# A hybrid decoder's gelus: square, tanh and VectorE steps replaced by ScalarE's gelu function

## The chip, the cores and the metric

One core of one Trainium2 chip runs the kernel. The metric is the device time of one execution in microseconds; the times below are medians of several executions. All matmuls and all vector work are in float32 (a first part of the first layer uses a split into two float32r halves).

## The reference

Two layers, each on 512 tokens of width 1024. Cut to what the change touches:

```python
h  = rg_lru(causal_conv(xr, ...), ...)          # recurrent branch
yr = h * jax.nn.gelu(gr)                        # gr: its gate branch
...
act = jax.nn.gelu(jnp.einsum('cd,ced->ce', xc, uc))   # 128 experts of each token
out = jnp.einsum('ce,ced->cd', gc * act, vc)          # gc: softmax over the chosen scores
```

`jax.nn.gelu` is here the tanh form, 0.5 x (1 + tanh(sqrt(2/pi) (x + 0.044715 x^3))). For each token and each of 8 heads a product-key search chooses 16 of 16384 experts; an expert is one row of `peer_u` and one row of `peer_v`. Around these stand differential attention (8 heads), two LayerNorms per layer (their square roots on ScalarE), softmax exponentials and sigmoids (computed as tanh).

## The kernel before, in words

Tokens lie in 4 blocks of 128 partitions. Three generators are merged into one program order by a clock of due times in `run` (L897 to L913): `gathers` walks the experts of every layer and block, `dense` walks the mixer and the routing of the four plans (a layer and a pair of blocks each, `PLAN`), and `late` chooses the experts of each plan's second block. Within the mixer `weave` alternates attention with the recurrent branch. The steps are emitted in that order; the framework may then place instructions of one engine a little earlier or later, and each engine runs its own queue in order.

`experts` (L785) takes two experts at a time (G=2, "a pair", 64 pairs per block and layer, 512 in all). For each expert GpSimd gathers 128 rows of u and v (L831, 1 MB per gather) into one of 8 buffers of the tag "uv", and VectorE multiplies the u half with x and sums it into one column of `dots` (L834, which also multiplies by C_GELU). After the second of the pair, ScalarE squares both columns (L842) and takes a tanh of each column by itself (L844, since scale and bias of that tanh are the column of `dots`); VectorE multiplies `dots` with the gate `g` into `w` (L846). The first step of the next pair then calls `finish` (L792): VectorE makes `w = (q + 1) * w` (L794), and each of the two experts is added either by VectorE into `acc` (L801) or by TensorE into `pv`, which needs a diagonal matrix made by ScalarE (L805) and two matmuls (L807, four in the trace). The buffer of an expert is free only after that, and the next gather into it waits for this.

Which of the two engines adds an expert is chosen by `Load`, a planner that sums a modelled cost of every emitted instruction for TensorE, VectorE and the DMAs: VectorE if `dve + 1.22 <= pe + 1.72`. It counts a VectorE instruction as 0.15 + n/960 us, n its elements per partition.

`lru` (L461) does a group of 128 channels in each of 8 turns per plan: conv, gates by tanh (L492), a tanh and an exp (L498, L499), a square root (L505), a scan (L516), and then the gelu of the gate branch: square (L520), a VectorE step (L521), tanh (L523), a VectorE step (L524) and the product with the scan's result (L527).

`choose` (L732) ends with a softmax over the chosen 16: exp (L773), sum, reciprocal, a factor 0.5/C_GELU (L777), product into `g`.

ScalarE evaluates functions from a table that holds some functions at a time; a change of table is an instruction of its own in the trace, ACT_TABLE_LOAD, shown at the line of the operation that it stands before.

Of the kernel before, what the change touches and what calls it, by code (L numbers as in the profile page):

```python
# [12 lines left out]
F32 = mybir.dt.float32  # L13
# [4 lines left out]
AF = mybir.ActivationFunctionType  # L18
ALU = mybir.AluOpType
AX = mybir.AxisListType  # L20

P = 128
D = 1024
# [10 lines left out]
LN_EPS = 1e-5  # L34
RMS_EPS = 1e-6
NEG = -1.0e30
C_GELU = math.sqrt(2.0 / math.pi)
A_GELU = math.sqrt(0.044715)


CH_Q, CH_K, CH_V, CH_XR, CH_GR, CH_GA, CH_GB = 0, 8, 16, 24, 32, 40, 48
# [81 lines left out]
class Decoder:  # L123
# [337 lines left out]
    def lru(self, l, cst, blocks, x, yr):  # L461
        nc, t1, t2 = self.nc, self.t1, self.t2
        n = len(blocks) * P
        t0 = blocks[0] * P
        c, hb, sp4 = cst["c"], cst["hb"], cst["sp4"]
        W = MAXN
        cost = len(blocks) * C_CHUNK
        for g in range(KC):
            gw = t2.tile([P, 2, P], F32, name="gw", tag="gs")
            nc.sync.dma_start(gw, self.gpk[l, g].rearrange("p (a c) -> p a c", a=2))  # L470
            px = self.proj_T(l, CH_XR + g, x, n)
            xr = t1.tile([P, 3 + W], F32, name="xr", tag="xr")
            if t0 == 0:
                nc.vector.memset(xr[:, 0:3], 0.0)
            else:
                nc.vector.tensor_copy(xr[:, 0:3], self.hist[:, g, :])
            nc.scalar.copy(xr[:, 3 : 3 + n], px[:, :n])
            yield cost
            nc.vector.tensor_copy(self.hist[:, g, :], xr[:, n : n + 3])
            xc = t1.tile([P, W], F32, name="xc", tag="xc")[:, :n]  # L480
            tap = lambda k: c[:, CC_W + k * 8 + g : CC_W + k * 8 + g + 1]
            nc.scalar.activation(xc, xr[:, 0:n], AF.Identity, bias=c[:, CC_B + g : CC_B + g + 1],
                                 scale=tap(0))
            for k in range(1, 4):
                nc.vector.scalar_tensor_tensor(out=xc, in0=xr[:, k : k + n], scalar=tap(k), in1=xc,
                                               op0=ALU.mult, op1=ALU.add)
            tha = t1.tile([P, W], F32, name="tha", tag="tha")[:, :n]
            thx = t1.tile([P, W], F32, name="thx", tag="thx")[:, :n]
            for gi, th in enumerate((tha, thx)):
                pg = self.ps_mm.tile([P, 512], F32, name="pg", tag="mm")  # L490
                nc.tensor.matmul(pg[:, :n], gw[:, gi, :], xc, start=True, stop=True)
                nc.scalar.activation(th, pg[:, :n], AF.Tanh, scale=0.5,  # L492
                                     bias=hb[:, gi * 8 + g : gi * 8 + g + 1])
            yield 1.0
            pgr = self.proj_T(l, CH_GR + g, x, n)
            s4 = sp4[:, g : g + 1]
            tl = t1.tile([P, W], F32, name="tl", tag="tl")[:, :n]
            nc.scalar.activation(tl, tha, AF.Tanh, scale=s4, bias=s4)  # L498
            nc.scalar.activation(tha, tha, AF.Exp, scale=s4, bias=s4)  # L499
            mu = t1.tile([P, W], F32, name="mu", tag="mu")[:, :n]  # L500
            nc.scalar.activation(mu, tha, AF.Square)

            nc.vector.scalar_tensor_tensor(out=mu, in0=mu, scalar=1.0, in1=tl, op0=ALU.add,
                                           op1=ALU.mult)
            nc.scalar.activation(mu, mu, AF.Sqrt, scale=-1.0)  # L505
            if t0 == 0:
                nc.vector.memset(mu[:, 0:1], 1.0)
            yield cost
            nc.vector.scalar_tensor_tensor(out=thx, in0=thx, scalar=1.0, in1=xc, op0=ALU.add,
                                           op1=ALU.mult)  # L510
            nc.vector.scalar_tensor_tensor(out=mu, in0=thx, scalar=0.5, in1=mu, op0=ALU.mult,
                                           op1=ALU.mult)
            hh = thx
            if t0 == 0:
                nc.vector.memset(self.hst[:, g : g + 1], 0.0)
            nc.vector.tensor_tensor_scan(hh, tha, mu, self.hst[:, g : g + 1], ALU.mult, ALU.add)  # L516
            nc.vector.tensor_copy(self.hst[:, g : g + 1], hh[:, n - 1 : n])
            yield 0.5
            pg = pgr
            nc.scalar.activation(tl, pg[:, :n], AF.Square, scale=A_GELU)  # L520
            nc.vector.scalar_tensor_tensor(out=tl, in0=tl, scalar=1.0, in1=pg[:, :n], op0=ALU.add,  # L521
                                           op1=ALU.mult)
            nc.scalar.activation(tl, tl, AF.Tanh, scale=C_GELU)  # L523
            nc.vector.scalar_tensor_tensor(out=tl, in0=tl, scalar=1.0, in1=pg[:, :n], op0=ALU.add,  # L524
                                           op1=ALU.mult)
            y = tl if yr.split else yr.plain[:, g, :n]
            nc.vector.scalar_tensor_tensor(out=y, in0=tl, scalar=0.5, in1=hh, op0=ALU.mult,  # L527
                                           op1=ALU.mult)
            if yr.split:
                self.keep(yr, (slice(None), g, slice(0, n)), y)  # L530
            yield 1.0
# [200 lines left out]
    def choose(self, l, h0, HG, sv, si, b):  # L732

        nc, t2 = self.nc, self.t2
# [36 lines left out]
        st = t2.tile([P, max(HGS[False])], F32, name="sm_st", tag="sm_st")[:, :HG]  # L771
# [1 line left out]
        nc.scalar.activation(ef, ef, AF.Exp)  # L773
        nc.vector.tensor_reduce(st, ef, AX.X, ALU.add)
        nc.vector.reciprocal(st, st)

        nc.vector.tensor_scalar(st, st, 0.5 / C_GELU, None, ALU.mult)  # L777
        nc.vector.tensor_tensor(self.g[b][:, js].rearrange("p (h k) -> p h k", h=HG), ef,
                                st.unsqueeze(2).to_broadcast([P, HG, TOPK]), ALU.mult)
        for h in range(h0, h0 + HG):  # L780
# [4 lines left out]
    def experts(self, l, b, G=2):  # L785
        nc, pp = self.nc, self.pp
        x = self.xn[b]
        pv = None
        e, g = self.e[b], self.g[b]
        began = [False]  # L790

        def finish(j0, q, w, uvs):  # L792

            nc.vector.scalar_tensor_tensor(out=w, in0=q, scalar=1.0, in1=w, op0=ALU.add,  # L794
                                           op1=ALU.mult)
            for i in range(G):
                j, t = j0 + i, uvs[i]
                self.load.update()
                vector = self.load.dve + 1.22 <= self.load.pe + 1.72
                if j == P - 1 or (vector and j < P - 2):  # L800
                    nc.vector.scalar_tensor_tensor(out=acc, in0=t[:, D:], scalar=w[:, i : i + 1],  # L801
                                                   in1=acc, op0=ALU.mult, op1=ALU.add)
                else:
                    dg = pp.tile([P, P], F32, name="dg", tag="dg")
                    nc.scalar.activation(dg, self.ident, AF.Copy, scale=w[:, i : i + 1])  # L805
                    for half in range(2):
                        nc.tensor.matmul(pv[:, half], dg,  # L807
                                         t[:, D + half * 512 : D + (half + 1) * 512],
                                         start=not began[0], stop=j == P - 2)
                    began[0] = True  # L810
            yield

        prev = iter(())
        for j0 in range(0, P, G):
# [8 lines left out]
                    pv = self.ps_v.tile([P, 2, 512], F32, name="pv", tag="pv")  # L823
            dots = pp.tile([P, G], F32, name="dots", tag="dots")
            q = pp.tile([P, G], F32, name="q", tag="q")
            w = pp.tile([P, G], F32, name="w", tag="w")
            uvs = []
            for i in range(G):
                j = j0 + i
                t = self.gp.tile([P, 2 * D], F32, name="uvt", tag="uv")  # L830
                nc.gpsimd.indirect_dma_start(  # L831
                    out=t, out_offset=None, in_=self.uv,
                    in_offset=bass.IndirectOffsetOnAxis(ap=e[:, j : j + 1], axis=0))
                nc.vector.scalar_tensor_tensor(out=t[:, :D], in0=t[:, :D], scalar=C_GELU, in1=x,  # L834
                                               op0=ALU.mult, op1=ALU.mult,
                                               accum_out=dots[:, i : i + 1])
                uvs.append(t)
                if i == 0:
                    next(prev, None)
                else:  # L840

                    nc.scalar.activation(q, dots, AF.Square, scale=A_GELU / C_GELU)  # L842
                    for k in range(G):
                        nc.scalar.activation(q[:, k : k + 1], q[:, k : k + 1], AF.Tanh,  # L844
                                             scale=dots[:, k : k + 1], bias=dots[:, k : k + 1])
                    nc.vector.tensor_tensor(w, dots, g[:, j0 : j0 + G], ALU.mult)  # L846
                yield 1
            prev = finish(j0, q, w, uvs)
        for _ in prev:
            pass  # L850
        sums = pp.tile([P, 1], F32, name="sums2", tag="sums2")
# [96 lines left out]
```

## Time and profile before

| | |
|---|---|
| median of 3 runs | 3462.6 us (3461.32 to 3471.1) |
| profiled execution's own time | 3468.77 us |
| its span in the trace | 3466.6 us |
| TensorE busy | 2996.7 us (86%) |
| VectorE busy | 2717.2 us (78%) |
| ScalarE busy | 1329.1 us (38%) |
| GpSimd busy (issue of gathers) | 1303.2 us (38%) |
| moved by DMA | 1290.65 MB, 372 GB/s over the span |
| chain that ended last | PE 36%, DVE 25%, DMA 19%, issue 9%, ACT 5%, POOL 5% |

PE is TensorE, DVE VectorE, ACT ScalarE, POOL GpSimd, SP the queue of plain DMAs. Busy time is the union of an engine's instructions. The chain that ended last is followed back from the last instruction, at each step to what released it. An average over the span hides that the work has stages with different limits, so the rows below are read stage by stage.

In this document the stages go by their place in the span: the **first projections** (0 to 300 us, before the first gather), three **attention stages** (460 to 720, 1150 to 1500, 2000 to 2300), three **routing stages** (1000 to 1150, 1750 to 1900, 2600 to 2800), and **streaming stages**, mostly the rest, the longest of them the last (2800 to the end).

### The profile page before, as it was taken

How to read it: one execution, taken by the hardware profiler on the slowest of the kernel's cores; microseconds unless marked ns; L12 is line 12 of the kernel's file. 1: busy time of each engine (PE TensorE's matmuls, PEld its weight loads, DVE VectorE, ACT ScalarE, POOL GpSimd, SP SyncE). 2: the span in 40 equal slices, each digit the busy share in tenths (PEclk: the TensorE clock that was granted, in tenths of full speed). 3: DMA queues.
4: the chain of work that ended last, by engine and by line, in shares of the span. 5: the costliest groups of instructions: out<-in, count | busy, mean ns of one | idle time of the engine just before them, and what ended most of it. 6: DMA issues, size and time to landing. Idle time of an engine off the chain costs nothing.

```text
span 3466.6 us, 39937 instructions
## 1 busy us (share of the span) xinstructions
PE 2996.7 (86%) x11916; PEld 1916.2 (55%) x11916; DVE 2717.2 (78%) x7210; ACT 1329.1 (38%) x3730; POOL 1303.2 (38%) x1033
## 2 busy tenths in 40 slices
PE   8997999999997899999997799999998687656555
PEld 7996666667754466677653266677765232212111
DVE  7765888888689677777799668878779965678777
ACT  7852245543132344533222345444232233223222
POOL 0001233334333333344433433334433345555553
PEclk9998999999999899999998999999999889877777
DMA  6455899999999999999999999999999899999997
GB/s 203 161 173 208 318 407 383 395 418 418 418 394 373 368 383 375 399 416 408 418 403 345 404 384 384 391 412 418 418 416 352 315 385 421 422 422 405 422 422 317
DMA packets 219126, 1290.65 MB, mean 372 GB/s; under 512 B 24592, under 2 KB 37136, under 8 KB 87840
## 3 DMA queue, kind: packets, MB, share of 16 engines
q0 software_dynamic: 147456, 1073.81, 76.7%
q1 hardware_dynamic: 71456, 214.30, 16.3%
q8 instruction: 96, 1.57, 0.2%
q14 instruction: 118, 0.97, 0.1%
HBM read 1285.92 MB, written 2.10 MB: 372 GB/s over the span
## 4 chain that ended last, share of the span: by engine, by line
PE 36%; DVE 25%; DMA 19%; issue 9%; ACT 5%; POOL 5%; POOLq 0%; SPq 0%; DVEq 0%; ACTq 0%
DMA uvt<-uv_dram,e 19%; PE ps_mm L255 14%; PE pv L807 13%; DVE uvt L834 9%; POOL uvt L831 5%; DVE acc L801 4%; PE ps_mm L277 2%; ACT q L844 1%; PE ps_mm L665 1%; DVE oh L765 1%; PE ps_ln L315 1%; DVE ef L767 1%; DVE oh L762 1%; PE s L388 1%; PE po L419 1%
## 5 line engine op out<-in xcount | busy, mean ns | idle before, releaser
L831 POOL DMA_INDIRECT uvt<-uv_dram,e x1024 | 1300.6, 1270 | 2132.0 <-PE pv L807 721.5
L807 PE MATMUL pv<-uvt,dg 128*128 128x512 f32 x2796 | 1448.5, 657 | 355.2 <-ACT dg L805 352.6
L834 DVE SCALAR_TENSOR_TENSOR uvt<-uvt,xn 128x1024 f32<-128x1024 f32 x1024 | 1243.2, 1219 | 151.3 <-DMA uvt<-uv_dram,e 89.2
L807 PEld LDWEIGHTS pv<-uvt,dg 128*128 128x128 f32 x2796 | 541.2, 205 | 1081.3 <-ACT dg L805 576.9
L255 PE MATMUL ps_mm<-room_xT,w 128*128 128x256 f32 x2304 | 538.4, 381 | 0.7 <-ACT room_xT L287 0.7
L842 ACT ACTIVATE q<-dots 128x2 f32<-128x2 f32 x512 | 103.7, 202 | 1093.4 <-DVE uvt L834 1088.3
L255 PEld LDWEIGHTS ps_mm<-room_xT,w 128*128 128x128 f32 x2304 | 431.4, 190 | 107.1 <-issue 50.3
L801 DVE SCALAR_TENSOR_TENSOR acc<-uvt,w,acc 128x1024 f32<-128x1024 f32 x325 | 416.6, 1282 | 7.8
L805 ACT ACTIVATE dg<-ident,w 128x128 f32<-128x128 f32 x699 | 263.0, 397 | 261.8 <-DVE w L794 154.5
L844 ACT ACTIVATE q<-q,dots 128x1 f32<-128x1 f32 x1024 | 341.9, 379 | 15.1
L794 DVE SCALAR_TENSOR_TENSOR w<-q,w 128x2 f32<-128x2 f32 x512 | 80.8, 158 | 289.8 <-ACT q L844 279.0
L665 PE MATMUL ps_mm<-room_xT,w 128*128 128x256 f32 (+1 forms) x1056 | 243.5, 379 | 0.0
L665 PEld LDWEIGHTS ps_mm<-room_xT,w 128*128 128x128 f32 x1056 | 196.5, 196 | 46.2 <-issue 23.8
L240 DVE TENSOR_TENSOR wsp<-raw,wsp 128x1024 fp32r<-128x1024 f32 x80 | 97.1, 1221 | 23.4 <-ACT wsp L239 23.2
L277 PEld LDWEIGHTS ps_mm<-w,room_xT 128*128 128x128 f32 x768 | 92.1, 192 | 9.0 <-issue 8.0
L277 PE MATMUL ps_mm<-w,room_xT 128*128 128x128 f32 x768 | 94.5, 276 | 0.0
L277 PEld LDWEIGHTS ps_mm<-w,room_m 128*128 128x128 f32 x768 | 89.2, 192 | 9.6 <-issue 8.6
L846 DVE TENSOR_TENSOR w<-dots,g 128x2 f32<-128x2 f32 x512 | 80.1, 157 | 17.3 <-ACT dg L805 4.3
L315 PE MATMUL ps_ln<-lnrows,ident 16*128 16x512 f32 x96 | 63.1, 779 | 35.3 <-DVE w L846 22.6
L255 PE MATMUL ps_mm<-room_yr,w 128*128 128x256 f32 x384 | 90.6, 380 | 0.0
L277 PE MATMUL ps_mm<-w,room_m 128*128 128x128 f32 x768 | 89.7, 275 | 0.4 <-DVE mth L544 0.2
L255 PE MATMUL ps_mm<-room_ya,w 128*128 128x256 f32 x384 | 88.9, 379 | 0.0
(200 smaller groups left out, 3023.6 us busy)
## 6 DMA issues: line engine op xcount, KB each, us to landing
w<-wpk_dram SPq DMA_DIRECT2D x304, 512.0 KB
raw<-wpk_dram SPq DMA_DIRECT2D x80, 512.0 KB
uvt<-uv_dram,e POOLq DMA_INDIRECT x1024
gw<-gpk_dram SPq DMA_DIRECT2D x32, 128.0 KB
sk<-spk_dram SPq DMA_DIRECT2D x64, 64.0 KB
xn<-x_dram SPq DMA_DIRECT2D x4, 512.0 KB
out_dram<-xn SPq DMA_DIRECT2D x8, 256.0 KB
lq<-lqk_dram SPq DMA_DIRECT2D x2, 128.0 KB
```

The source lines that it names most:

```text
L240: self.nc.vector.tensor_tensor(lo, raw, hi.bitcast(F32), ALU.subtract)
L255: self.nc.tensor.matmul(ps[:, :n], w, x, start=i == 0, stop=i == len(steps) - 1)
L277: self.nc.tensor.matmul(out[:, i], x(slice(i * P, (i + 1) * P)), w, start=j == 0, stop=j == len(steps) - 1)
L315: self.nc.tensor.matmul(ps[:, half], self.ident[:16, r : r + 1].to_broadcast([16, P]), self.lnrows, start=True, stop=True)
L665: nc.tensor.matmul(pq[:, :n], w[:, kc, :], self.acts_x.plain[:, kc, t0 : t0 + n], start=kc == 0, stop=kc == KC - 1)
L801: nc.vector.scalar_tensor_tensor(out=acc, in0=t[:, D:], scalar=w[:, i : i + 1], in1=acc, op0=ALU.mult, op1=ALU.add)
L805: nc.scalar.activation(dg, self.ident, AF.Copy, scale=w[:, i : i + 1])
L807: nc.tensor.matmul(pv[:, half], dg, t[:, D + half * 512 : D + (half + 1) * 512], start=not began[0], stop=j == P - 2)
L831: nc.gpsimd.indirect_dma_start(out=t, out_offset=None, in_=self.uv, in_offset=bass.IndirectOffsetOnAxis(ap=e[:, j : j + 1], axis=0))
L834: nc.vector.scalar_tensor_tensor(out=t[:, :D], in0=t[:, :D], scalar=C_GELU, in1=x, op0=ALU.mult, op1=ALU.mult, accum_out=dots[:, i : i + 1])
L842: nc.scalar.activation(q, dots, AF.Square, scale=A_GELU / C_GELU)
L844: nc.scalar.activation(q[:, k : k + 1], q[:, k : k + 1], AF.Tanh, scale=dots[:, k : k + 1], bias=dots[:, k : k + 1])
```

## The change

In the experts, one gelu over both columns takes the place of the square and the two tanh; `w` becomes the plain product of that with `g`, made in `finish`. In the recurrent branch one gelu takes the place of square, VectorE step, tanh and VectorE step. The factors that belonged to the old form go (C_GELU in the dot product becomes 1.0, and the softmax loses its 0.5/C_GELU step).

```diff
@@ lru
-            pg = pgr
-            nc.scalar.activation(tl, pg[:, :n], AF.Square, scale=A_GELU)
-            nc.vector.scalar_tensor_tensor(out=tl, in0=tl, scalar=1.0, in1=pg[:, :n], op0=ALU.add,
-                                           op1=ALU.mult)
-            nc.scalar.activation(tl, tl, AF.Tanh, scale=C_GELU)
-            nc.vector.scalar_tensor_tensor(out=tl, in0=tl, scalar=1.0, in1=pg[:, :n], op0=ALU.add,
-                                           op1=ALU.mult)
+            nc.scalar.activation(tl, pgr[:, :n], AF.Gelu_apprx_tanh)
             y = tl if yr.split else yr.plain[:, g, :n]
-            nc.vector.scalar_tensor_tensor(out=y, in0=tl, scalar=0.5, in1=hh, op0=ALU.mult,
-                                           op1=ALU.mult)
+            nc.vector.tensor_tensor(y, tl, hh, ALU.mult)
@@ choose
-        nc.vector.tensor_scalar(st, st, 0.5 / C_GELU, None, ALU.mult)
@@ experts
-        def finish(j0, q, w, uvs):
-            nc.vector.scalar_tensor_tensor(out=w, in0=q, scalar=1.0, in1=w, op0=ALU.add,
-                                           op1=ALU.mult)
+        def finish(j0, q, uvs):
+            w = pp.tile([P, G], F32, name="w", tag="w")
+            nc.vector.tensor_tensor(w, q, g[:, j0 : j0 + G], ALU.mult)
...
-            w = pp.tile([P, G], F32, name="w", tag="w")
...
-                nc.vector.scalar_tensor_tensor(out=t[:, :D], in0=t[:, :D], scalar=C_GELU, in1=x,
+                nc.vector.scalar_tensor_tensor(out=t[:, :D], in0=t[:, :D], scalar=1.0, in1=x,
...
-                    nc.scalar.activation(q, dots, AF.Square, scale=A_GELU / C_GELU)
-                    for k in range(G):
-                        nc.scalar.activation(q[:, k : k + 1], q[:, k : k + 1], AF.Tanh,
-                                             scale=dots[:, k : k + 1], bias=dots[:, k : k + 1])
-                    nc.vector.tensor_tensor(w, dots, g[:, j0 : j0 + G], ALU.mult)
+                    nc.scalar.activation(q, dots, AF.Gelu_apprx_tanh)
...
-            prev = finish(j0, q, w, uvs)
+            prev = finish(j0, q, uvs)
```

## Rows read from the trace of the kernel before

**Rows 1.** Busy time by stage: stretch, length, each engine's busy us (instructions), clock, DMA share, GB/s.

```profile
0.00:300.00 300.00, 278.09 (x2168) 264.00 (x2169) 205.45 (x498) 191.92 (x378) 3.66 (x10) 0.98 0.47 158
...
460.00:720.00 260.00, 252.58 (x1105) 173.71 (x1104) 224.14 (x555) 136.72 (x373) 102.22 (x83) 1.00 0.99 396
...
1000.00:1150.00 150.00, 121.71 (x401) 72.14 (x400) 145.35 (x574) 43.66 (x151) 55.28 (x45) 0.93 0.94 365
1150.00:1500.00 350.00, 338.64 (x1262) 213.46 (x1260) 251.19 (x678) 165.21 (x475) 125.65 (x112) 0.97 0.98 389
...
1750.00:1900.00 150.00, 118.92 (x406) 72.17 (x405) 148.50 (x572) 41.51 (x144) 55.18 (x43) 0.90 0.96 375
...
2000.00:2300.00 300.00, 295.40 (x1203) 195.03 (x1202) 239.75 (x604) 149.91 (x415) 115.28 (x94) 1.00 0.99 390
...
2600.00:2800.00 200.00, 150.32 (x408) 77.56 (x407) 192.32 (x704) 54.84 (x184) 79.01 (x62) 0.88 0.88 333
2800.00:3466.00 666.00, 419.02 (x683) 142.62 (x682) 482.37 (x893) 186.89 (x567) 334.33 (x252) 0.82 0.98 405
```

**Rows 2.** Page, the span in 40 equal slices: GB/s of the DMAs.

```profile
GB/s 203 161 173 208 318 407 383 395 418 418 418 394 373 368 383 375 399 416 408 418 403 345 404 384 384 391 412 418 418 416 352 315 385 421 422 422 405 422 422 317
```

**Rows 3.** Chain of waits by line, in 50:150, 460:720, 1150:1500, 1750:1900, in that order.

```profile
by line: PE ps_mm L255 21.0%; PE ps_mm L277 12.1%; PE ps_qk L255 10.1%; ACT wsp L239 9.5%; PE pg L491 5.2%; ACT L523 4.4%; ACT pr L400 4.2%; ACT L505 3.8%; PE s L388 2.4%; DVE xc L485 2.3%; issue 2.0%; ACT xc L482 2.0%; PE po L419 1.8%; ACT
by line: DMA uvt<-uv_dram,e 38.8%; PE pv L807 10.7%; PE ps_mm L255 9.4%; issue 9.3%; DVE uvt L834 7.9%; DVE acc L801 4.7%; PE ps_mm L277 2.7%; POOL uvt L831 2.3%; DVE at_st L397 1.6%; DVE oh L762 1.5%; DVE oh L765 1.1%; PE s L388 1.1%; DVE 
by line: PE pv L807 39.7%; PE ps_mm L255 25.7%; PE ps_mm L277 6.4%; DVE uvt L834 4.0%; PE pg L491 3.0%; PE s L388 2.2%; DMA uvt<-uv_dram,e 2.1%; ACT q L844 1.3%; PE po L419 1.2%; issue 1.1%; DVE xc L485 0.9%; DVE oh L762 0.8%; DVE oh L765 0
by line: DVE uvt L834 31.7%; DVE acc L801 12.4%; issue 8.1%; DVE sc L730 4.8%; DVE si L727 4.8%; DVE top L727 4.7%; DVE sv L725 3.4%; DVE top L725 3.3%; DVE ef L767 3.3%; DVE ca L745 2.8%; PE pv L807 2.6%; PE ps_mm L665 2.3%; ACT q L844 2.2
```

**Rows 4.** Groups by line: busy us, mean ns of one, idle before and what ended it.

```profile
L842 ACT ACTIVATE q<-dots 128x2 f32<-128x2 f32 x512 | 103.7, 202 | 1093.4 <-DVE uvt L834 1088.3 <-issue 3.5 <-DVE mu L507 0.9
L844 ACT ACTIVATE q<-q,dots 128x1 f32<-128x1 f32 x1024 | 341.9, 379 | 15.1
L846 DVE TENSOR_TENSOR w<-dots,g 128x2 f32<-128x2 f32 x512 | 80.1, 157 | 17.3 <-ACT dg L805 4.3 <-issue 2.6 <-DVE uvt L834 0.2
L523 ACT ACTIVATE tl<-tl 128x256 f32<-128x256 f32 x32 | 13.2, 414 | 5.8 <-DVE tl L521 5.4
L801 DVE SCALAR_TENSOR_TENSOR acc<-uvt,w,acc 128x1024 f32<-128x1024 f32 x325 | 416.6, 1282 | 7.8
```

**Rows 5.** The largest group of table loads, of 102 in all.

```profile
L505 ACT ACT_TABLE_LOAD x32 | 41.1, 1283 | 0.6
```

**Rows 6.** ScalarE's timeline, 2104 to 2109: start, us, line, operation, idle before.

```profile
2104.84 0.59 ACT L499 ACTIVATE tha<-tha,sp 128x256 f32<-128x256 f32 x1
...
2106.07 0.20 ACT L842 ACTIVATE q<-dots 128x2 f32<-128x2 f32 x1 [0.19 <-DVE uvt L834]
...
2106.99 1.28 ACT L505 ACT_TABLE_LOAD   x1
2108.28 0.42 ACT L505 ACTIVATE mu<-mu 128x256 f32<-128x256 f32 x1
```

**Rows 7.** Timeline at the end of the span, ScalarE and VectorE.

```profile
3456.47 1.28 ACT L334 ACT_TABLE_LOAD   x1
3456.49 0.15 DVE L331 TENSOR_SCALAR ln_st<-ln_st 128x1 f32<-128x1 f32 x1 [1.31 <-ACT acc L329]
```

**Rows 8.** Pieces of the chain of waits: start, us, what. Loads, and one run of matmuls.

```profile
52.16 1.28 ACT L523
...
277.25 1.28 ACT L334
...
1167.98 1.28 ACT L334
...
1169.59 1.28 ACT L844
...
1183.65 3.43 PE pv L807 x8
```

More of the change, by code (lines that the diff above doesn't have):

```diff
@@ L36 @@
 NEG = -1.0e30
-C_GELU = math.sqrt(2.0 / math.pi)
-A_GELU = math.sqrt(0.044715)
 CH_Q, CH_K, CH_V, CH_XR, CH_GR, CH_GA, CH_GB = 0, 8, 16, 24, 32, 40, 48
```

## The prediction

> **What bounds the kernel now.** I read the busy times by stage first, then the chain of waits of each stage, then the groups by line, and last ScalarE's timeline. No single engine bounds the span. In the long last stage the DMAs are the limit: the slices with nothing but gathers move 418 to 422 GB/s and never more [rows 2], and TensorE and VectorE are well under their stretch there [rows 1]. In the attention stages TensorE is busy 97 to 98% (338.64 of 350, 295.40 of 300) with the DMAs at 389 to 396 GB/s [rows 1], and TensorE's lines hold 78% of the chain of the second one (39.7 + 25.7 + 6.4 + 3.0 + 2.2 + 1.2); in the first attention stage DMA holds 38.8% and TensorE only 24% (10.7 + 9.4 + 2.7 + 1.1) [rows 3]. In the routing stages VectorE is busy 96 to 99% [rows 1] and holds 71% of the chain (31.7 + 12.4 + 4.8 + 4.8 + 4.7 + 3.4 + 3.3 + 3.3 + 2.8) [rows 3]. In the first projections ScalarE is on the chain: its tanh L523 alone has 4.4%, its root L505 3.8% [rows 3]. ScalarE is nowhere full after that, and before the 512 squares it sat waiting, 1088.3 us in total, for the dot products [rows 4]. So what ScalarE saves in busy time is worth little by itself; what counts is TensorE in the attention stages, VectorE in the routing stages, and every table load that lands on a chain.
>
> **Table loads.** The gelu takes 512 squares' place at about their 202 ns and removes 1024 tanh of 379 ns, 341.9 us of ScalarE [rows 4]. What it adds is loads. The trace shows exp and tanh sharing a table, and the square root needing another: a load of 1283 ns stands before each of 32 roots [rows 5], 102 in all. I walked ScalarE's operations in order, once with the table rule of today (101 loads come out, each at the line where the trace has it; the first is the start-up load), and once with a gelu in the place of each square, in a table of its own beside exp's. The stretch in rows 6 shows the pattern: an exp, then the square of the experts 0.64 us behind it, then a root; with a gelu in the middle, that is one load more. If the gelu's table also holds tanh, 279 loads come out; if not, 367. If the gelu shared exp's table it would be 99. No row shows which. The rows have two of this kernel's functions in one table, so I take 279; 367 differs almost only in streaming stages. By stage the walk gives, before and after: first projections 20 and 29, the attention stages 50 and 147 together, the routing stages none and 31.
>
> A load doesn't wait for the operand of the function behind it: the one at 3456.47 starts before VectorE's step on that operand ends at 3456.64 [rows 7]. So a load before an expert's gelu goes into ScalarE's wait for the dots. How many loads reach a chain? In the first projections 8 of 20, from the one at 52.16 to the one at 277.25; in the attention stages 2 of 50, at 1167.98 and 1169.59, both at a LayerNorm [rows 8]. That is a share of 0.40 where ScalarE is on the chain and of 0.04 where it isn't; between these ends, both from rows, lies the whole uncertainty.
>
> The load is 1.28 us in the rows, and the operation behind it starts at once (2106.99 + 1.28, next at 2108.28) [rows 6]. The Trainium skill, page "ScalarE: Activation LUTs", section "What ACT_TABLE_LOAD costs", speaks of about 2.66 us for every switch, a drain of 1.38 us included; with that price my two load terms would grow and the sum below would be -2 us, so no change. The row shows no such drain, and the row decides.
>
> **The sum.**
> - First projections: 9 loads more are 11.5 us, 8 tanh of 414 ns less [rows 4] are 3.3 us; 8.2 us at the share 0.40 give **+3.3 us**. The VectorE steps that go there are not on the chain.
> - Attention stages, TensorE. The planner counts 0.152 us less of VectorE for each pair and 0.417 us less for each of 16 recurrent steps per stage. GpSimd's instructions give 41, 56 and 47 pairs (half of 83, 112 and 94) [rows 1]: 12.9, 15.2 and 13.8 us. It evens this out by moving experts from TensorE to VectorE, each moving the balance by 1.22 + 1.72 us: 4.4, 5.2 and 4.7 experts. Two experts are 3.43 us of matmul [rows 8], so TensorE loses 7.6, 8.9 and 8.1 us. With the chain's shares of 24% and twice 78% that is **-15.1 us**. The DMAs leave room for it (389 to 396 against 418 GB/s).
> - Attention stages, loads: 97 x 1.283 = 124.5 us, at 0.04: **+5.0 us**.
> - Routing stages: 75 pairs (half of 45, 43 and 62) [rows 1] lose L846 at 157 ns [rows 4], 11.8 us, of which 71% is 8.4. The planner gives back 75 x 0.152 / 2.94 = 3.9 experts of 1.282 us [rows 4], 3.5 us at 71%. 31 new loads are 39.8 us; VectorE waits there for little that ScalarE makes, but the exps of the softmax come among its steps, so I take 0.10, nearer the lower end: 4.0. Together **-0.9 us**. L777 is left out as a small gain.
> - The tanh in the pair's own chain: L844 has 1.3% of 350 us and 2.2% of 150 us in two stages [rows 3], 4.6 + 3.3. With one operation left this goes: **-7.9 us**. Next late is then the dot product itself.
> - Streaming stages: nothing, the DMA rate hides it; were that cover gone, the 0.76 us per pair would show as a gain. At the very end the last pair saves 0.76: **-0.8 us**.
>
> Sum -16.4 us: 3468.8 becomes 3452.4 for the profiled execution, which stood 6.2 us over the median, so **3446 us** in the median.
>
> **The rivals.** *Loads stand in line (slower).* Exps of attention and gelus of experts alternate in ScalarE's queue; everything behind a load, diagonals for TensorE (L805) and copies that free PSUM among it, comes 1.28 us later, and twice in a row where an exp follows. If the share is 0.40 in the attention and routing stages too, the 164.3 us of new loads there cost 65.7 instead of 9.0: +40 us, 3503. It decides from a share of 15% on (no gain) and is a measurable loss from 22%. For it: the first projections' share. Against it: pairs of loads around roots stand in today's attention stages, and none of them is on the chain. The skill's same page, section "Table sets: the hidden batching unit", asks to group calls by set for just this cost; the 2 of 50 speak against the rule deciding here.
>
> *The attention stages are held by the DMAs.* Their share is 0.97 to 0.99 busy already [rows 1], and the first one's chain is DMA. Then the TensorE term and that stage's 4.6 us don't come: +3.3 us, 3466, no change. Against it: 418 GB/s elsewhere with the same gathers.
>
> *The change adds no loads*, since the gelu shares exp's table: without the load terms -30 us, 3433. No row excludes it. [...]
>
> **How the numbers follow.** A difference of 0.3% (10.4 us) is about what a measurement of this kernel can tell from none. I give the forecast 0.40 (its own range 3432 to 3460, so 0.29 faster and 0.11 same), the loads in line 0.25 (0.21 slower, 0.04 same), the DMA-bound case 0.25 (0.20 same, 0.03 faster, 0.02 slower), no loads 0.10 (faster). Together faster 0.42, same 0.35, slower 0.23. The range's lower end is the forecast with the full 24.6 us of TensorE and no load cost after the first projections, 3427, rounded down; its upper end is loads in line at a share of 0.32, 3446 + 44 (52.6 in place of 9.0), 3490.
>
> **What would show it.** The groups must show about 280 loads of 1283 ns, over half of the new ones at L400, L773, L499 and the experts' gelu, mostly without idle time charged to them. The attention stages should be 3 to 9 us shorter each with some 15 more experts on VectorE in them and TensorE still on the chain; the routing stages should keep their length. I am wrong if loads turn up on the chain in the attention or routing stages in number (30 of them would eat the gain there), if those stages keep their length while TensorE's busy time falls, or if the loads stay near 100.

## The result: 3445 us, and the profile after

The changed kernel takes 3445.14 us in the median of 8 runs, the kernel before 3466.94 us beside it: a ratio of 0.9939, 95% interval [0.9929, 0.9949]. The forecast was 3446 us. The profiled execution's span went from 3466.6 to 3441.3 us. Three lines of its page: the span, busy time by engine, and the shares of the chain that ended last.

```profile
span 3441.3 us, 38208 instructions
...
PE 2962.3 (86%) x11832; PEld 1899.5 (55%) x11832; DVE 2660.9 (77%) x6622; ACT 1242.6 (36%) x2851; POOL 1307.3 (38%) x1033
...
PE 44%; DVE 24%; DMA 19%; issue 6%; POOL 3%; ACT 3%; POOLq 0%; SPq 0%; DVEq 0%; ACTq 0%
```

TensorE, VectorE and ScalarE all do less, and TensorE's part of the chain has grown from 36 to 44%. Groups by line of the changed kernel (busy us, mean ns, idle before and its releaser) answer to [rows 4] and [rows 5]:

```profile
L829 ACT ACTIVATE q<-dots 128x2 f32<-128x2 f32 x512 | 104.1, 203 | 1132.3 <-DVE uvt L822 1117.4 <-DVE e L761 5.1 <-DVE ln_st L325 4.5
...
L829 ACT ACT_TABLE_LOAD x115 | 147.5, 1283 | 19.6 <-DVE uvt L822 17.0 <-DVE at_st L402 0.6
...
L398 ACT ACT_TABLE_LOAD x64 | 82.1, 1283 | 1.1
...
L784 DVE TENSOR_TENSOR w<-q,g 128x2 f32<-128x2 f32 x512 | 80.7, 158 | 208.9 <-ACT q L829 203.9 <-issue 3.3 <-ACT dg L794 1.3
...
L790 DVE SCALAR_TENSOR_TENSOR acc<-uvt,w,acc 128x1024 f32<-128x1024 f32 x346 | 443.6, 1282 | 7.9
```

The gelu costs what the square cost (203 against 202 ns). Loads rise from 102 to 300: 115 before the experts' gelu, 64 before the exp of attention's softmax, and 121 at ten other lines. The planner puts 346 experts on VectorE instead of 325.

To see where the time went, the two traces must be cut at the same work, not at the same time. I cut them at the ends of the same dot products (L834 before, L822 after), numbers 48 to 140, 218 to 262, 262 to 352, 440 to 486, 530 to 610 and 704 to 768 of 1024, counted from 0: attention, routing, attention, routing, attention, routing. Busy time by stage, columns as in [rows 1], of the kernel before:

```profile
488.50:785.20 296.70, 287.39 (x1270) 197.66 (x1270) 255.37 (x598) 151.19 (x415) 114.58 (x94) 1.00 0.99 399
1045.50:1181.00 135.50, 105.00 (x275) 52.91 (x274) 124.18 (x476) 43.77 (x135) 50.41 (x43) 0.89 0.94 364
1181.00:1479.20 298.20, 291.59 (x1115) 187.97 (x1115) 215.77 (x603) 144.68 (x416) 103.20 (x93) 0.98 0.98 387
1762.60:1915.00 152.40, 119.97 (x375) 68.80 (x374) 150.00 (x578) 42.05 (x144) 56.35 (x45) 0.88 0.94 364
2037.10:2296.50 259.40, 254.88 (x1054) 168.91 (x1054) 217.00 (x550) 130.78 (x365) 101.01 (x82) 1.00 0.99 390
2600.70:2805.80 205.10, 155.42 (x416) 79.23 (x414) 195.56 (x711) 56.11 (x188) 80.46 (x64) 0.88 0.89 335
```

The same six stretches of the changed kernel:

```profile
487.80:777.50 289.70, 286.00 (x1285) 200.81 (x1284) 255.92 (x547) 169.67 (x355) 121.98 (x95) 1.00 1.01 410
1039.60:1170.50 130.90, 96.76 (x234) 45.79 (x233) 115.17 (x391) 38.49 (x93) 51.21 (x42) 0.90 0.93 360
1170.50:1460.90 290.40, 280.39 (x1087) 182.39 (x1086) 212.87 (x548) 167.40 (x355) 111.30 (x92) 0.98 0.99 395
1750.80:1897.50 146.70, 112.86 (x349) 64.32 (x348) 145.92 (x532) 36.56 (x102) 56.24 (x44) 0.87 0.93 359
2019.20:2276.50 257.30, 252.75 (x1067) 169.24 (x1066) 216.03 (x506) 159.69 (x323) 101.40 (x82) 1.00 1.00 398
2581.00:2781.70 200.70, 148.79 (x400) 75.38 (x400) 193.25 (x659) 54.86 (x138) 79.28 (x64) 0.88 0.90 340
```

The attention stages are 7.0, 7.8 and 2.1 us shorter, with ScalarE busier by 18 to 29 us in each, DMAs at 395 to 410 instead of 387 to 399 GB/s and VectorE hardly changed. The routing stages are 4.6, 5.7 and 4.4 us shorter. The first dot product ends 1.8 us later. The streaming stretches give some 5 us back. Each trace is one execution, and a shorter stage is not yet a gain, as the recurrent branch alone will show.

### The profile page after: what moved, and what is told of

It reads as the page before. It is cut to its first block, busy times and chain, and to the rows that moved or that the text cites. A ratio compares the mean times of both kernels' runs of the same rounds, so it can differ in the third digit from the quotient of the medians.

```text
span 3441.3 us, 38208 instructions
## 1 busy us (share of the span) xinstructions
PE 2962.3 (86%) x11832; PEld 1899.5 (55%) x11832; DVE 2660.9 (77%) x6622; ACT 1242.6 (36%) x2851; POOL 1307.3 (38%) x1033
## 3 DMA queue, kind: packets, MB, share of 16 engines
q1 hardware_dynamic: 71456, 214.30, 16.4%
## 4 chain that ended last, share of the span: by engine, by line
PE 44%; DVE 24%; DMA 19%; issue 6%; POOL 3%; ACT 3%; POOLq 0%; SPq 0%; DVEq 0%; ACTq 0%
DMA uvt<-uv_dram,e 19%; PE ps_mm L253 18%; PE pv L796 16%; DVE uvt L822 8%; POOL uvt L819 3%; DVE acc L790 3%; PE ps_mm L275 3%; PE ps_ln L313 1%; PE ps_qk L253 1%; DVE oh L756 1%; DVE ef L758 1%; PE s L386 1%; DVE oh L753 1%; PE ps_mm L656 1%; PE po L417 1%
## 5 line engine op out<-in xcount | busy, mean ns | idle before, releaser
L796 PE MATMUL pv<-uvt,dg 128*128 128x512 f32 x2712 | 1417.4, 662 | 379.3 <-ACT dg L794 377.8
L822 DVE SCALAR_TENSOR_TENSOR uvt<-uvt,xn 128x1024 f32<-128x1024 f32 x1024 | 1243.8, 1220 | 248.3 <-DMA uvt<-uv_dram,e 244.4
L796 PEld LDWEIGHTS pv<-uvt,dg 128*128 128x128 f32 x2712 | 527.8, 206 | 1094.7 <-ACT dg L794 604.4
L790 DVE SCALAR_TENSOR_TENSOR acc<-uvt,w,acc 128x1024 f32<-128x1024 f32 x346 | 443.6, 1282 | 7.9
L784 DVE TENSOR_TENSOR w<-q,g 128x2 f32<-128x2 f32 x512 | 80.7, 158 | 208.9 <-ACT q L829 203.9
L829 ACT ACT_TABLE_LOAD x115 | 147.5, 1283 | 19.6 <-DVE uvt L822 17.0
L237 ACT CAST wsp<-raw 128x1024 fp32r<-128x1024 f32 x80 | 82.7, 1052 | 14.8 <-PE ps_mm L253 7.8
L822 DVE DVE_READ_ACCUMULATOR uvt<-uvt,xn 128x1 f32 x1024 | 84.1, 82 | 0.0
```

Of the source, the lines that this page charges most:

```text
L237: self.nc.scalar.copy(hi, raw)
L784: nc.vector.tensor_tensor(w, q, g[:, j0 : j0 + G], ALU.mult)
L796: nc.tensor.matmul(pv[:, half], dg, t[:, D + half * 512 : D + (half + 1) * 512], start=not began[0], stop=j == P - 2)
L829: nc.scalar.activation(q, dots, AF.Gelu_apprx_tanh)
```

## The experiments

Twelve kernels, each timed in five rounds beside the kernel before, which had medians of 3467.23, 3467.47 and 3468.58 us in the three lots. The changed kernel stands at 0.9939. "Shares" are the planner's choice of engine for each expert: old 325 and new 346 on VectorE. Across lots a difference is given by the medians or by the ratios, which can differ by some 3 us.

| kernel | median us | ratio to before, 95% interval |
|---|---|---|
| experts only | 3455.18 | 0.9958 [0.9945, 0.9971] |
| recurrent branch only | 3471.60 | 1.0008 [0.9999, 1.0018] |
| changed, old shares | 3456.96 | 0.9971 [0.9960, 0.9982] |
| before, new shares | 3466.04 | 0.9989 [0.9981, 0.9998] |
| changed, tanh for gelu (no added loads) | 3434.68 | 0.9908 [0.9894, 0.9922] |
| before, one tanh (short pair chain) | 3467.23 | 0.9998 [0.9990, 1.0007] |
| before, without L846 | 3464.33 | 0.9989 [0.9981, 0.9998] |
| before, loads only | 3481.21 | 1.0043 [1.0031, 1.0056] |
| before, VectorE steps out, new shares | 3459.60 | 0.9976 [0.9966, 0.9987] |
| before, VectorE steps out, old shares | 3462.37 | 0.9982 [0.9973, 0.9991] |
| changed, tanh for gelu, old shares | 3459.59 | 0.9974 [0.9964, 0.9983] |
| changed, planner with 0.13 | 3441.45 | 0.9922 [0.9909, 0.9936] |

### The two halves of the change

Experts only: the recurrent branch of the kernel before is put back.

```diff
-            nc.scalar.activation(tl, pgr[:, :n], AF.Gelu_apprx_tanh)
+            nc.scalar.activation(tl, pg[:, :n], AF.Square, scale=A_GELU)
...
+            nc.scalar.activation(tl, tl, AF.Tanh, scale=C_GELU)
...
```

> Only the experts' gelu is changed; the recurrent branch keeps square, tanh and its VectorE steps. The planner now puts 340 experts on VectorE (before 325, changed kernel 346). Theory A, the sum of the prediction: without the recurrent branch the first projections cost nothing more, TensorE's relief in the attention stages is about half (144 pairs x 0.152 / 2.94 = 7.4 experts, -8 us), the tanh in the pair's chain goes in full (-8 us), loads +5: about 3467 - 13 = 3454 us. Theory B, the gain is the shorter chain of a pair and nothing else: all of it is here, 3445 us. Theory C, the gain is the work taken from VectorE and ScalarE in the recurrent branch: 3465 us.

Recurrent branch only: the opposite, `experts` and `choose` as before.

```diff
-            nc.scalar.activation(tl, pg[:, :n], AF.Square, scale=A_GELU)
...
+            nc.scalar.activation(tl, pgr[:, :n], AF.Gelu_apprx_tanh)
```

> Only the recurrent branch's gelu is changed; the experts keep square, two tanh and two VectorE steps. The planner puts 331 experts on VectorE (before 325). Theory A: +3 us in the first projections, TensorE relieved by 6 experts or 10 us of which some 7 count, a few loads: about 3467 - 4 = 3463 us. Theory B: no gain, 3467 us or up to 3 more. Theory C: most of the gain, 3447 us.

Measured 3455.2 and 3471.6 us. The first is the 3454 of theory A, though its single terms, tried below, don't hold. The second, 2.8 us over the kernel before by the ratio and 4.4 by the medians, is nearest theory B. The halves don't add: alone, the recurrent branch gives nothing or a loss of up to 0.2%; on top of the experts' half it is worth 7 us by the ratios and 10 by the medians (3455.2 to 3445.1). That was the first sign that the gain is not a sum of terms.

The trace of the recurrent branch alone also warns of reading stages as gains. Cut at the same dot products, its attention stages are 10.1 us and its routing stages 4.6 us shorter than before, and yet its span is 1.1 us longer: the first dot product ends 2.9 us later, and the streaming stretches give 12.9 us back.

### The shares alone, and the change without them

Both kernels take the engine of each expert from a fixed list of 1024 bits instead of the planner.

```diff
-                vector = self.load.dve + 1.22 <= self.load.pe + 1.72
+                vector = SHARES[(l * NB + b) * P + j] == "1"
```

> The changed kernel, with the engine of each of the 1024 experts fixed to what the planner chose in the kernel before (325 on VectorE, not 346). Theory A: the term of TensorE's relief (-15 us) is gone, 3445 + 15 = 3460 us. Theory B (the pair's shorter chain): the shares don't matter, 3445 us, within 4.

> The kernel before in every operation, with the engine of each expert fixed to the changed kernel's choice (346 on VectorE, not 325). Theory A: TensorE's relief comes without the gelu, -15 us, less some 3 us for VectorE in the routing stages: 3467 - 12 = 3455 us. Theory B: no gain, 3467 us or a little more, since VectorE has not been relieved.

With the old shares the changed kernel takes 3457.0 us: 11 to 12 us, over half the gain, hang on the moved experts, near theory A's 15. But the moved experts by themselves give the kernel before only 0.11%, 1 to 4 us, where theory A expected 12. So TensorE's relief is real and needs something else of the change.

### The price of the loads

One kernel has all of the change but a function of exp's table, the other has the loads and nothing else.

```diff
-                    nc.scalar.activation(q, dots, AF.Gelu_apprx_tanh)
+                    nc.scalar.activation(q, dots, AF.Tanh)
```

> The changed kernel with a plain tanh where the gelu stands, in the experts and in the recurrent branch: the same instructions and the same 346 experts on VectorE, but the function shares exp's table, so that some 100 loads are left of 295. It leaves out the gelu (its output is another). Theory A, the loads cost what the prediction's three load terms say, 3 + 5 + 4 us: 3445 - 12 = 3433 us. Theory B, the loads cost what stands on the changed kernel's chain, 25 pieces of 1.28 us: 3445 - 32 = 3413 us. Theory C, they are hidden: 3445 us, within 4.

```diff
-                    nc.scalar.activation(q, dots, AF.Square, scale=A_GELU / C_GELU)
+                    nc.scalar.activation(q, dots, AF.Gelu_apprx_tanh, scale=A_GELU / C_GELU)
```

(and the same two edits in the recurrent branch).

> The kernel before with the gelu function in the place of its two squares and everything behind them kept (so the polynomial's square is left out): only table loads are added, to about 280 to 295. Theory A: the three load terms, 3467 + 12 = 3479 us. Theory B, loads that come on top of the two tanh lengthen the pair's chain and stand in line: 3467 + 32 = 3499 us. Theory C: hidden, 3467 us.

Without the added loads 3434.7 us, 10.5 under the changed kernel, with 100 loads in its trace; loads alone (313 in the trace) make the kernel before 0.43% or 14.9 us slower. Theory A said 12 for both. In the tanh kernel's trace the load group at the experts' function has shrunk from 115 to

```profile
L829 ACT ACT_TABLE_LOAD x25 | 32.1, 1283 | 0.4
```

In the changed kernel 25 loads stand on the chain, whole or cut, which would be up to 32 us by their durations; a third of that is what they cost. That the next-latest thing is not far behind when a load goes would explain it, but is not shown. None of the 25 lies inside a routing stage, 16 lie in the attention stages. The traces of the changed and the tanh kernel, cut at the same dot products, put the cost elsewhere: without the loads the first dot product ends 5.0 us sooner and the streaming stretches are 15.0 us shorter, while the attention and routing stages are 6.3 and 4.1 us longer. A stretch of the changed kernel's chain of waits (start, us, what) in an attention stage shows a pattern that makes up 8 of those 16:

```profile
2108.53 1.28 ACT L829
2109.81 0.01 issue
2109.82 0.20 ACT q L829
2110.03 0.02 issue
2110.04 1.28 ACT L398
2111.33 0.01 issue
2111.34 0.82 ACT pr L398 x2
```

Here a gelu has been placed between the two exps of one softmax (the first exp ran at 2107.35): a load for the gelu, a load back for the second exp. 12 of the 64 softmaxes are cut like this, 11 by a gelu of the experts and one by a gelu of the recurrent branch.

### Which part makes room for the moved experts?

The changed kernel does two other things for VectorE: fewer small steps, and a `q` that comes sooner, as ScalarE does one operation for it and not a square and two tanh. Below, ScalarE's chain of a pair is long with a square and two tanh, and short with one operation, or with a square and one tanh. Each alone, on the kernel before:

```diff
-                    for k in range(G):
-                        nc.scalar.activation(q[:, k : k + 1], q[:, k : k + 1], AF.Tanh,
-                                             scale=dots[:, k : k + 1], bias=dots[:, k : k + 1])
+                    nc.scalar.activation(q, q, AF.Tanh)
```

> The kernel before with one tanh over both columns instead of two with the column as scale and bias; it leaves out that factor. Loads, VectorE's work and the shares stay as before; the pair's chain on ScalarE falls from 202 + 2 x 379 to some 400 ns. Theory A: three quarters of the pair-chain term of 8 us, 3467 - 6 = 3461 us. Theory B, the pair's chain is the main thing in the gain: 3467 - 15 = 3452 us. Theory C: it is hidden, 3467 us.

```diff
-                    nc.vector.tensor_tensor(w, dots, g[:, j0 : j0 + G], ALU.mult)
```

> The kernel before without the product of dots and g (L846, 512 times 157 ns); finish takes g in its place, so that the factor dots is left out. Shares fixed as before, loads as before. Theory A, VectorE's small steps count in the routing stages alone: 3467 - 8 = 3459 us. Theory B: they lie beside other work or overlap, 3467 us. Theory C, VectorE's order in the attention stages is eased too: 3450 us.

The short chain alone gives nothing (0.9998), against theory A's 6 us and B's 15. The missing product gives 0.11%, under half of theory A's 8 us. Then all of the change's VectorE steps taken out (L846, L521, L524, L777), ScalarE's operations kept, with new and with old shares:

```diff
-            nc.vector.scalar_tensor_tensor(out=tl, in0=tl, scalar=1.0, in1=pg[:, :n], op0=ALU.add,
-                                           op1=ALU.mult)
...
-        nc.vector.tensor_scalar(st, st, 0.5 / C_GELU, None, ALU.mult)
...
-                    nc.vector.tensor_tensor(w, dots, g[:, j0 : j0 + G], ALU.mult)
```

> The kernel before without the VectorE steps that the change removes (the product L846, the two steps of the recurrent gelu, L777; their factors are left out), with the changed kernel's 346 experts on VectorE. ScalarE keeps squares and both tanh, and no table load is added. Theory D, the gain needs VectorE's relief and the moved experts together, and no shorter pair chain: some 30 us under the kernel before (10 us of loads under the changed kernel), 3437 us. Theory E, it needs the short chain as well: about the sum of the single effects, 3467 - 4 - 2 - a few = 3458 us.

> The same as the run before it in this list, with the old 325 experts on VectorE. Theory D: VectorE's relief alone does little, 3467 - 8 = 3459 us or above, 15 to 20 us behind the run with the new shares. Theory E: the shares make 2 to 4 us of difference here, as they did without the relief: 3460 us, beside 3458.

3459.6 and 3462.4: theory E, within 3 us in both. With the long chain kept, the new shares are worth 2 to 3 us, within the noise, even when VectorE has been relieved. The last cell, everything but the new shares and without loads:

> The changed kernel with tanh in place of the gelu (no added loads) and the old 325 experts on VectorE; it leaves out the gelu. With the new shares this was 3435 us. The changed kernel itself lost 12 us with the old shares. If shares and loads add up: 3435 + 12 = 3447 us. If the loads are only dear where TensorE is the bound, the old shares cost more here: 3452 us.

3459.6 us, well off both expectations. Beside the 3434.7 us with new shares, the moved experts are worth 23 to 25 us here; and beside the changed kernel with old shares (3457.0) the loads cost nothing. So shares and loads don't add either: with the short chain the loads show only together with the new shares. It is no rule that old shares hide loads, as with the long chain they cost the kernel before 0.43%.

The last four kernels without VectorE's steps and without added loads make a square. Long chain: 3462.4 us with old shares, 3459.6 with new. Short chain: 3459.6 and 3434.7. Neither the chain nor the shares alone bring more than 3 us; both together bring 26 to 28. Cut at the same dot products, the new shares shorten the attention stages by 17.6 us with the short chain (861.3 to 843.7), and with the long one they do not (847.0 and 848.7).

What the engines wait for (engine, line, waited for: us in total, times, longest) fits this in part. Each list is of one execution. The kernel before:

```profile
POOL uvt L831 <- PE pv L807: 721.5, 340, 11.9
POOL uvt L831 <- DVE acc L801: 695.3, 273, 9.6
...
DVE w L794 <- ACT q L844: 279.0, 288, 7.2
...
DVE uvt L834 <- DMA uvt<-uv_dram,e: 89.2, 86, 3.5
```

The kernel before with VectorE's steps out, old shares:

```profile
DVE w L795 <- ACT q L845: 352.6, 310, 7.5
```

The kernel before with new shares only:

```profile
POOL uvt L837 <- DVE acc L807: 779.8, 294, 9.5
POOL uvt L837 <- PE pv L813: 657.2, 320, 11.7
...
DVE w L800 <- ACT q L850: 295.4, 294, 7.3
...
DVE uvt L840 <- DMA uvt<-uv_dram,e: 58.2, 63, 2.8
```

The kernel before with one tanh:

```profile
POOL uvt L831 <- PE pv L807: 722.2, 345, 11.7
...
DVE uvt L834 <- DMA uvt<-uv_dram,e: 232.9, 261, 2.9
DVE w L794 <- ACT q L843: 182.7, 283, 7.3
```

The changed kernel:

```profile
POOL uvt L819 <- PE pv L796: 655.1, 352, 10.4
POOL uvt L819 <- DVE acc L790: 614.5, 247, 10.2
...
DVE uvt L822 <- DMA uvt<-uv_dram,e: 244.4, 244, 3.2
DVE w L784 <- ACT q L829: 203.9, 291, 7.5
```

The changed kernel with tanh for gelu, old shares:

```profile
POOL uvt L825 <- PE pv L802: 781.5, 398, 11.0
...
POOL uvt L825 <- DVE acc L796: 531.7, 218, 9.8
```

The same with new shares:

```profile
POOL uvt L819 <- PE pv L796: 703.1, 368, 11.1
POOL uvt L819 <- DVE acc L790: 603.1, 252, 9.0
```

With the long chain VectorE stands still for `q` 279 to 353 us. Take its own steps away and it waits 74 us longer for `q` at the same place: little is won (0.18%). Take experts off TensorE and VectorE waits less for data (89 to 58) and more for `q` (279 to 295); GpSimd, whose gathers need free buffers, waits 64 us less for TensorE and 84 us more for VectorE: little is won. Shorten the chain alone and VectorE's wait moves from `q` (279 to 183) to the data (89 to 233 us), while the gathers wait for TensorE as long as before (722 us): nothing is won. With the short chain, in the tanh kernels, the moved experts take 78 us from GpSimd's wait for TensorE and add 71 us for VectorE, so that the balance turns.

A reading that fits is two limits in a row, each hiding the other: with the long chain VectorE can't take over experts without holding up the gathers itself. The waits don't prove it. In the changed kernel VectorE's two waits (204 and 244 us) are about those of one tanh alone, GpSimd's 655 us for TensorE stand in the kernel with new shares only as well (657), and 7 us of balance are few beside some 25 us of gain. That chain and shares pay only together is shown by the times; through which wait is not.

### One step further

> The changed kernel with 0.13 in place of 0.15 us per VectorE instruction in the planner's count: 358 instead of 346 experts on VectorE, 10 of the 12 in the attention stages. Correct output. Theory A, TensorE bounds these stages and VectorE has room: 10 experts are 17 us of matmul, at the chain's shares of the prediction about -11 us, 3434 us. Theory F, VectorE has no more room or the DMAs bound: 3445 us, or up to 5 more.

```diff
-                self.dve += 0.15 + n / 960
+                self.dve += 0.13 + n / 960
```

3441.5 us, 0.9922 [0.9909, 0.9936] against the changed kernel's 0.9939 [0.9929, 0.9949]: the fastest kernel here that leaves nothing out, but the intervals overlap: the step from 346 to 358 experts is worth 4 to 6 us by medians and ratios, if it is anything, and not the 11 of theory A. The first step, of 21 experts, gave 11 to 12.

## Why the prediction was right, and where its steps were not

The forecast of 3446 us is within 1 us of the measured median, and that closeness is luck: the kernel before has a median 4.3 us higher in eight runs than in the three shown before the prediction, and the gain was 5.4 us larger than forecast. The change was forecast at -16.4 us and measured at -21.8: right in direction, a quarter short. What carries the gain was named rightly, TensorE's relief by moved experts less a modest price of loads; that the terms stand by themselves was wrong. By term:

- **Loads** (+4.6 of the first term, +5.0, +4.0): held in their sum. 279 were counted and 300 came; 13.6 us were forecast, 10.5 measured between the changed kernel and the tanh kernel, 14.9 on the kernel before, and nothing with short chain and old shares. Their places were off: in the attention stages 16 of 168 loads stand on the chain, 0.10 and not 0.04, and none of 34 in the routing stages, not 0.10. In the traces the 5.0 us at the first dot product agree with the first term, while the rest shows in the streaming stretches, where the sum has nothing. The argument that no pair of loads around a root was on the chain before misread its own row, since the two at 1167.98 and 1169.59 stand around a LayerNorm's root. The Trainium skill ("ScalarE: Activation LUTs", "What ACT_TABLE_LOAD costs") gives about 2.66 us per switch, of which 1283 ns are the load itself. All 300 loads take 1283 ns; no row shows the rest, and the sum by that price (it would raise three load terms, not two), no change, didn't come. The rival of loads in line is out, as its price was 66 us, and so is the rival without added loads.
- **TensorE's relief** (-15.1): held in size within the changed kernel. The planner moved 4, 4 and 4 experts in the three stages (forecast 4.4, 5.2, 4.7), and fixing the old shares costs 11 to 12 us. The step that failed is the silent one, that the term stands by itself: alone it is 1 to 4 us. The rival that the DMAs hold these stages is out: their rate rose in all three, and the gain that it forbids came.
- **The pair's chain** (-7.9): failed as a term. "With one operation left this goes" is true of the chain of waits, where 1.3% of a stage was read as time to be won. Shortened alone, it won nothing; VectorE's wait moved to the data. It is instead the condition under which TensorE's relief pays: the same new shares bring 23 to 25 us with it and 2 to 3 without it.
- **Routing stages** (-0.9, with 3.3 of the pair's chain): failed in size, they lost 14.7 us. TensorE's busy time in these stretches falls by 6.6 to 8.2 us in the rows above; the prediction read only VectorE's 71% of the chain and gave TensorE no part in it. Whether its relief is what shortens them is not shown: with old shares the changed kernel, cut the same way, loses 2.0 us there, but with tanh for gelu and old shares 9.3. The cause stays open.
- **First projections** (+3.3): +1.8 us at the first dot product. **Streaming** (0): some 5 us were given back there; the stretch right behind the second attention stage alone is 6.5 us longer, at 414 GB/s of the DMAs.
- **The sum**: the terms of the attention stages, the pair's chain included, gave -14.7 us and the stages lost 16.9; the routing stages were forecast 10 us too small, streaming 5 us too good. By the recurrent branch's trace, such errors partly belong together: what a stage saves, streaming can give back. Adding terms was itself the weakest step. Single effects of the twelve kernels don't add up to the change: one tanh 0.02%, new shares 0.11%, VectorE's steps 0.18%, loads -0.43% would make a loss of 0.12%, while together they gain 0.61%.

Open: the short chain with new shares but with VectorE's old steps was not run, so how much of the gain needs those steps too is not shown. The kernels in which chain and shares pay also do one operation of ScalarE in place of two in the recurrent branch, and that was not told apart from the pair's chain. The lists of shares also differ in which experts are moved (103 of 1024 decisions differ, for 21 net), and number and place were not told apart.

## What to carry to other kernels

When engines wait for each other in a ring of buffers, the time that one of them holds on the chain is not the time to be won by shortening it: ask where its wait goes, and try the two reliefs together as well as one by one. A planner that counts instructions turns a small saving on one engine into a relief of another, so a change of operations should be measured with the old shares too. A function in another table can pay although it triples the table loads, if most loads fall where the engine would be idle (here 198 loads more, 254 us by their durations, cost 0 to 15 us); look first for pairs of operations of one table that the order has pulled apart.

## What was not expected of the hardware

A load usually went ahead of the wait for the operand, as in [rows 7], but not always: the 115 loads before the experts' gelu show 19.6 us of idle time in front of them, 17.0 of it for the dots, and nearly all of it before 13 of them. In the stretch of the chain above, the queue waits for the dot product (to 2108.46), and the load begins after it, at 2108.53, so that its 1.28 us lie bare. And ScalarE can be busy some 18 to 29 us more in an attention stage of 260 to 300 us while the stage gets shorter.
